# Two placements in a planned kernel: broadcast loads tied to tiles of x, and the sums of squares of the convolution at a lower rank

## The chip, the cores and the metric

One NeuronCore of a Trainium2 chip runs the whole program. Five engines have queues of their own and run them in order: TensorE (PE, with its weight loads PEld), VectorE (DVE), ScalarE (ACT), GpSimd (POOL) and SyncE (SP). SP mostly issues DMAs; POOL and ACT issue some as well. The metric is the device time of one execution in microseconds (us). The kernel before has a median of 1287.59 us over three runs.

## The reference, cut to what matters

One decoder layer on 1024 tokens of width 1024 in float32: a token mixer (sparse attention with 8 heads beside a short convolution) and a squared-ReLU MLP.

```python
h = rms_norm(x, g_mix_norm)
z = h @ w_in
q, kc, vc, ks_, vs_, kw_, vw_, gl, hc, cg, bg = split(z)
q = rms_norm(q, g_q)
k_cmp = rms_norm(compress(kc, pe_cmp[0], w_cmp1[0], b_cmp1[0], w_cmp2[0], b_cmp2[0]), g_k[0])
v_cmp = compress(vc, pe_cmp[1], w_cmp1[1], b_cmp1[1], w_cmp2[1], b_cmp2[1])
k_slc, k_win = rms_norm(ks_, g_k[1]), rms_norm(kw_, g_k[2])
attn_out = nsa_attention(q, k_cmp, v_cmp, k_slc, vs_, k_win, vw_, sigmoid(gl))
conv_out = bg * causal_conv3(cg * hc, conv_w)
mixed = concat(rms_norm(attn_out, g_out[:512]), rms_norm(conv_out, g_out[512:]))
x = x + mixed @ w_o
h = rms_norm(x, g_ffn_norm)
x = x + square(relu(h @ w_up)) @ w_down
```

Three things matter below. The vectors `g_q`, `g_k`, `b_cmp1` and `b_cmp2` are needed on every partition, since tokens lie on partitions where they are applied. `rms_norm(conv_out)` needs, for each token, the sum of the squares of its 512 convolution channels; its reciprocal root can be applied after the product with `w_o`. And nothing of the attention needs the convolution.

## The kernel before

**A plan ahead of the program.** The kernel doesn't issue instructions as its code runs. Each call such as `nc.tensor.matmul(...)` makes a node in a list (`Plan.op`), with the nodes that it must follow (those that wrote or read the same parts of the same tiles), an estimated cost, and a running number `n.k`. Allocating a tile and opening or closing a pool are nodes too, without an engine. `Plan.schedule` then runs a simulation of the five engines over the list: a node is ready when all that it follows has ended, and an engine that comes free takes its ready node of the highest priority. The priority is the longest path of estimated costs behind the node, less 0.03 for each place in the list, plus `plan.plus` as it stood when the node was made. `Plan.issue` emits the instructions in the order that comes out. So the plan fixes the order in each engine's queue. The waits on the chip are made from the tiles that instructions really share: an edge that exists only in the list moves an instruction in its queue, and nothing on the chip waits for it.

Tiles with the same tag share a ring of buffers. When the last node on a tile has ended in the simulation, its buffer goes into a heap, ordered by that time, and the next tile of the ring takes the first. All emitted instructions carry line 267 in the profile, the line where `Plan.op` calls the engine, so the profile is read by the names of tiles.

**The start.** `x` is loaded in eight tiles `xts` of 128 tokens (512 KB each, on SP), among the first pieces of `w_in` (also 512 KB). `norm_in` squares and sums a tile on ACT, takes the reciprocal root on DVE and POOL (`rs_t`, `ri`), scales the tile on DVE, and PE transposes it into `hTh` and `hTl`, a high and a low part for products of nearly float32 accuracy (`mm3`: three matmuls for one). POOL issues four loads that spread a vector over all partitions: `gq_bc` and `gk_bc` are written at the head of the code (lines 625 and 626), `b1_bc` and `b2_bc` after the keys' projection (lines 700 and 701). `gk_bc` is read when the first keys are normed (`kn`), `gq_bc` when queries are, `b1_bc` and `b2_bc` in the compression. In the profile `b1_bc` and `b2_bc` share the name `b_bc`; the one of 64 KB is `b2_bc`, the one of 256 KB `b1_bc`.

**The convolution and what follows.** Channels lie on partitions. For each of four blocks of 128 channels, three products `zc` run over two halves of 512 tokens; the result `cv` goes into `MCh`/`MCl`, and its square is added into `sqs[0]` or `sqs[1]`, one for each half. For the last block squares and additions run on DVE. Then eight matmuls with a vector of ones sum the squares over partitions, one for each 128 tokens (`ssc`, four from each `sqs`; the profile names this buffer `s__2825` and counts two instructions for each, 16 in all). `rsqrt` makes `rconv` of it on DVE (`rs_t`) and POOL.

Behind that stand the products `wc` of the convolution's part with `w_o`: 16 sums of 12 matmuls each, two for each block of 128 tokens, in the order of `ORDER` (blocks 3, 2, 1, 0 from the first half first). They rotate over three PSUM banks (tags `ot`, `ot`, `ms`). DVE multiplies each by its column of `rconv` and adds it to a tile of x (the group `y<-wc,rconv,y`), which frees the bank. Between them `k_transposes` turns the keys (`tp<-ident,kn`, four transposes a tile, three banks `pt`), and ACT and DVE split them into `KH` and `KL`. `queries` loads q again (`qx`) and turns it. `b2z.close()` gives the memory of `sqs` back, and a tile of x takes it later.

Of the kernel before, what the change touches and what calls it, by code (L numbers as in the profile page):

```python
# [16 lines left out]
DRAM = bass.MemoryType.DRAM  # L17

P = 128
# [131 lines left out]
class Plan:  # L151
# [27 lines left out]
    def pool(self, **kw):  # L179
        outer = self  # L180

        class Pool:
            def __enter__(self):
                self.bases, self.real, self.bufs = [], None, kw.get("bufs", 1)
                self.dram = kw.get("space") == DRAM
                self.psum = kw.get("space") == PSUM
                self.node = outer.pool_node(self.enter)
                return self

            def enter(self):  # L190
                self.real_pool = outer.tc.tile_pool(**kw)
                self.real = self.real_pool.__enter__()

            def __exit__(self, *a):
                if outer.done:
                    self.real_pool.__exit__(None, None, None)
                else:
                    n = outer.pool_node(lambda: self.real_pool.__exit__(None, None, None))
                    for b in self.bases:
                        n.preds.update(x.k for x in b.nodes + [b.node])  # L200
                    self.bases = None

            def tile(self, shape, dtype, name, tag=None, bufs=None):
                k = dict(name=name)
                if tag is not None:
                    k["tag"] = tag
                if bufs is not None:
                    k["bufs"] = bufs
                b = Base(self, shape, dtype, k)
                ring = outer.rings.setdefault((id(self), tag or name), [bufs or self.bufs])  # L210
                b.ring, b.node = ring, outer.node(None, [self.node])
                b.node.base = b
                if len(ring) > 1:
                    b.node.preds.add(ring[-1].node.k)
                ring.append(b)
                outer.bases.append(b)
                self.bases.append(b)

                def make():
                    b.tile = self.real.tile(shape, dtype, **k)  # L220
                b.node.do.append(make)
                return View(b, b.shadow, ())
        return Pool()

    done = False
# [8 lines left out]
    def op(self, name, engine, method, a, kw):  # L234
        views = [("" if i else "out", v) for i, v in enumerate(a)] + list(kw.items())
        views = [(k, v) for k, v in views if isinstance(v, View)]
        preds, raw, touched = set(), set(), []
        for k, v in views:
            w = k in ("out", "accum_out")
            r0, r1, m = v.region()  # L240
            touched.append((v.base, w, r0, r1, m))
            assert v.base.pool.bases is not None, v.base.kw
            preds.add(v.base.node.k)
            for n, ow, o0, o1, om in v.base.seen:
                if (w or ow) and r0 < o1 and o0 < r1 and m & om:
                    preds.add(n.k)
                    if ow:
                        raw.add(n.k)
        out = views[0][1] if views else None
        if name == "PE":  # L250
            preds.update([n.k for n in out.base.nodes if n.engine == "PE"][-1:])
        last = self.last_pe if name == "PE" else None
        if (last is not None and last.out is out.base and len(last.do) < self.GROUP and method == "matmul" and
                all(p <= last.k for p in preds)):
            node = last
            preds.discard(node.k)
        else:
            node = self.node(name)
            node.out = out.base if out is not None else None
        node.preds |= preds  # L260
        node.raw |= raw
        if name == "PE":
            self.last_pe = node

        def real(x):
            return x.real() if isinstance(x, View) else x
        node.do.append(lambda: getattr(engine, method)(*[real(x) for x in a], **{k: real(x) for k, x in kw.items()}))  # L267
        for b, w, r0, r1, m in touched:
            if b not in node.bases:
                b.nodes.append(node)  # L270
                node.bases.append(b)
            if w:
                b.seen = [s for s in b.seen if not (r0 <= s[2] and s[3] <= r1 and s[4] & ~m == 0)]
            b.seen.append((node, w, r0, r1, m))
        busy, late, size = self.cost(name, method, a, kw, views)
        node.plus = self.plus
        node.late = node.busy + late
        node.busy += busy
        node.port = self.port
        node.bytes += size  # L280
        node.names = method + " " + " ".join(v.base.kw["name"] for _, v in views)
        return node

    last_pe = None
    plus = 0.0
    GROUP = 1

    def cost(self, name, method, a, kw, views):
# [47 lines left out]
    def schedule(self, weight=lambda n: -.03 * n.k, rings=True):  # L336
        nodes = self.nodes
        slots, held, left_of = {}, {}, {}
        for b in self.bases:
            slots[id(b.ring)] = [(0.0, i, {}) for i in range(b.ring[0])]  # L340
            held[id(b.ring)] = []
            left_of[b] = [len(b.nodes), 0.0, {}]
            b.last = {x[0].k for x in b.seen if not x[1]} or {x[0].k for x in b.seen}
        for n in nodes:
            n.succ, n.left, n.ready = [], len(n.preds), 0.0
        for n in nodes:
            for p in n.preds:
                nodes[p].succ.append(n)
# [32 lines left out]
        def settle(n, t):  # L381
            for s in n.succ:
                s.left -= 1
                s.ready = max(s.ready, t + (.05 if s.engine and n.engine and s.engine != n.engine else 0.0))
                if not s.left:
                    stack.append(s)

        while True:
            while stack:
                n = stack.pop()  # L390
                if n.engine is None:
                    if n.base is not None:
                        ring = id(n.base.ring)
                        if not slots[ring]:
                            held[ring].append(n)
                            continue
                        t, _, n.users = heapq.heappop(slots[ring])
                        n.ready = max(n.ready, t)
                    order.append(n)
                    settle(n, n.ready)  # L400
                else:
                    heapq.heappush(wait[n.engine], (n.ready, n.k))
            best = None
            for e in names:
                if ready[e]:
                    t = free[e]
# [50 lines left out]
            for b in n.bases:  # L457
                rest = left_of[b]
                rest[0] -= 1
                rest[1] = max(rest[1], done)  # L460
                if n.k in b.last:
                    rest[2][n.line] = n
                if not rest[0]:
                    heapq.heappush(slots[id(b.ring)], (rest[1], 9 + b.node.k, rest[2]))
                    stack.extend(held[id(b.ring)])
                    held[id(b.ring)] = []
            for s in n.succ:
                s.left -= 1
                own = s.engine == e and not n.bytes and (e == "PE" or n.k not in s.raw)
                s.ready = max(s.ready, free[e] if own else done + .05 * (s.engine is not None))  # L470
                if not s.left:
                    stack.append(s)
        return end, order
# [14 lines left out]
def trunk_layer(ctx, tc, x, g_mix_norm, w_in, g_q, g_k, pe_cmp, w_cmp1, b_cmp1, w_cmp2, b_cmp2,  # L488
# [123 lines left out]
    with ExitStack() as a:  # L612
# [9 lines left out]
        nc.sync.dma_start(rows[24:36], conv_w.rearrange("j (k p) -> (j k) p", p=P))  # L622
        nc.sync.dma_start(rows[36:68], pe_cmp.rearrange("k (q two) d -> (k q) (two d)", two=2))
        plan.plus = 0.0
        nc.gpsimd.dma_start(gq_bc, g_q.partition_broadcast(P))
        nc.gpsimd.dma_start(gk_bc, g_k.partition_broadcast(P))
        tp = psB.tile([P, 512], F32, name="tp", tag="tr", bufs=3)
        nc.tensor.transpose(tp[:, :68], rows, ident[:68, :68])
        nc.vector.tensor_copy(cols, tp[:, :68])
# [17 lines left out]
        norm_in(0)  # L647
        kv_pieces = w_chunk(C_KV, 512)
        for tb in range(2, NT):
            nc.sync.dma_start(xts[tb], x2d[tb * P:(tb + 1) * P])  # L650
        for tb in range(1, NT):
            norm_in(tb)

# [14 lines left out]
    with ExitStack() as b1:  # L668
# [28 lines left out]
        cp = pool(cs, "cp", side="right")  # L697
        b1_bc = cp.tile([P, 2, 256], F32, name="b1_bc")
        b2_bc = tlp.tile([P, 2, HD], F32, name="b2_bc")
        nc.gpsimd.dma_start(b1_bc, b_cmp1.partition_broadcast(P))  # L700
        nc.gpsimd.dma_start(b2_bc, b_cmp2.partition_broadcast(P))

        def compress_steps():
            for kv in range(2):
# [120 lines left out]
    with ExitStack() as b2:  # L825
# [175 lines left out]
            return Qs  # L1001

        ssc = psS.tile([P, 512], F32, name="s_")[:, :NT]
        for tb in range(NT):
            nc.tensor.matmul(ssc[:, tb:tb + 1], sqs[tb // 4][:, (tb % 4) * P:(tb % 4 + 1) * P], ones,
                             start=True, stop=True)
        rsqrt(rconv, ssc, NT, 1.0 / CW)
        b2z.close()
        pts = [pool(kp_stack, "pt0")]
# [495 lines left out]
```

## Time and profile before

| | us |
|---|---|
| runs | 1282.5, 1287.59, 1288.23 |
| the profiled execution | 1286.31 |
| its span, first to last instruction | 1284.2 |
| PE busy in it | 1241.2 |
| DVE, ACT, POOL busy | 898.5, 691.3, 681.3 |

The profile is of one execution. A group shows busy time, the mean of one instruction and the idle time ahead of it with what ended that (the releaser). The chain of waits is the way back from the last instruction, at each step to what released it. A view by stretches shows for each the busy time of each engine, the granted PE clock (1.00 is full), the share of the 16 DMA engines in use and the GB/s they moved. In a row of the timeline stand start, length, engine, operation, output and inputs, the count of merged instructions, and the idle time before with its releaser in brackets. Matmuls overlap, so the length of one, 0.39 us at 512 columns, is longer than the distance from one start to the next.

### The profile page before, as it was taken

What the parts mean: (1) busy time and instruction counts of PE and PEld (TensorE: products, weight loads), DVE (VectorE), ACT (ScalarE), POOL (GpSimd) and SP (SyncE); (2) the same over time, 40 slices, a digit from 0 to 9 for tenths busy, and PEclk for the clock granted to TensorE, in tenths of its full rate; (3) what the DMA queues carried; (4) which work ended last, traced back from release to release, by engine and by line L of the source; (5) the groups of instructions that cost most, each with busy time, mean ns of one, the idle gap of its engine ahead of it and who ended that gap; (6) DMA issues with size and microseconds to landing.
All of it is one profiled execution on the core that took longest, in us unless ns stands there. A gap on an engine that the chain in (4) does not pass through costs nothing.

```text
span 1284.2 us, 18498 instructions
## 1 busy us (share of the span) xinstructions
PE 1241.2 (97%) x6170; PEld 1026.9 (80%) x6170; DVE 898.5 (70%) x1805; ACT 691.3 (54%) x1514; POOL 681.3 (53%) x599
## 2 busy tenths in 40 slices
PE   6999999999989999999999999999999999999998
PEld 5898888877768878888778878888877787888886
DVE  5367884433598788988885656656657998887875
ACT  6345552111499888887966554554434444444440
POOL 2255512120133332221586777777787989878861
PEclk9999999998999999999999999999999999999999
DMA  6243341212220010000415344355339654444413
GB/s 217 83 119 131 124 123 50 73 35 82 99 83 34 34 34 34 26 18 1 132 35 195 124 163 136 135 172 163 132 134 381 201 186 158 161 134 129 152 47 131
DMA packets 91574, 147.66 MB, mean 115 GB/s; under 512 B 10900, under 2 KB 45800, under 8 KB 91480
## 3 DMA queue, kind: packets, MB, share of 16 engines
q1 hardware_dynamic: 88408, 138.70, 32.6%
q10 hardware_dynamic: 2304, 5.24, 1.1%
q0 software_dynamic: 768, 2.56, 0.7%
q8 instruction: 48, 0.79, 0.3%
q14 instruction: 46, 0.38, 0.1%
HBM read 102.43 MB, written 44.04 MB: 114 GB/s over the span
## 4 chain that ended last, share of the span: by engine, by line
PE 84%; DVE 5%; ACT 5%; DMA 4%; issue 2%; POOL 0%; SPq 0%; DVEq 0%; ACTq 0%; POOLq 0%
PE X L267 24%; PE Z L267 15%; PE zc L267 10%; PE zp L267 8%; PE tp L267 6%; PE ot L267 4%; PE wc L267 3%; PE wa L267 3%; PE W L267 3%; DMA wu<-in_w_up_dram 1%; PE ops L267 1%; DVE y L267 1%; PE hp L267 1%; ACT pt L267 1%; ACT wu L267 1%
## 5 line engine op out<-in xcount | busy, mean ns | idle before, releaser
L267 PE MATMUL X<-we,uu 128*128 128x512 f32 x768 | 193.2, 393 | 5.7 <-ACT uu L267 4.0
L267 PEld LDWEIGHTS X<-we,uu 128*128 128x128 f32 x768 | 144.5, 189 | 39.3 <-ACT uu L267 8.1
L267 PE MATMUL Z<-we,uu 128*128 128x512 f32 x576 | 147.4, 391 | 0.6 <-DVE y L267 0.6
L267 ACT ACTIVATE uu<-ur 128x512 fp32r<-128x512 f32 x112 | 69.1, 631 | 123.3 <-PE X L267 62.2
L267 PEld LDWEIGHTS Z<-we,uu 128*128 128x128 f32 x576 | 107.2, 188 | 25.9 <-DVE y L267 2.4
L267 PE MATMUL tp<-ident,pt 128*128 128x128 f32 x528 | 100.8, 273 | 2.2 <-ACT pt L267 1.3
L267 POOL TENSOR_TENSOR d<-d 128x512 f32<-128x512 f32 x64 | 96.3, 1525 | 12.5 <-DVE d L267 11.3
L267 DVE TENSOR_TENSOR pl<-tp,ph 128x512 fp32r<-128x512 f32 (+1 forms) x148 | 95.2, 655 | 7.7 <-ACT ph L267 7.3
L267 ACT ACTIVATE pt<-pt,nm 128x640 f32<-128x640 f32 (+7 forms) x128 | 93.9, 736 | 9.7 <-DVE nm L267 9.3
L267 ACT ACTIVATE ph<-tp 128x512 fp32r<-128x512 f32 (+1 forms) x148 | 82.8, 575 | 19.6 <-PE tp L267 13.9
L267 DVE TENSOR_TENSOR y<-X,y 128x512 f32<-128x512 f32 x128 | 79.6, 680 | 15.9 <-PE X L267 15.3
L267 ACT ACTIVATE w_hi<-w_raw,cols 128x128 fp32r<-128x128 f32 (+3 forms) x128 | 54.0, 490 | 66.1 <-PE zc L267 48.9
L267 POOL TENSOR_TENSOR uu<-ur,uu 128x512 fp32r<-128x512 f32 x56 | 78.3, 1403 | 15.2 <-DVE y L267 10.7
L267 DVE TENSOR_TENSOR we<-s,we 128x512 fp32r<-128x512 f32 x42 | 39.3, 935 | 59.0 <-ACT we L267 27.5
L267 DVE TENSOR_TENSOR uu<-ur,uu 128x512 fp32r<-128x512 f32 x56 | 66.2, 1187 | 20.1 <-ACT uu L267 19.1
L267 PEld LDWEIGHTS tp<-ident,pt 128*128 128x128 f32 x528 | 67.9, 140 | 13.9 <-ACT pt L267 2.7
L267 DVE SCALAR_TENSOR_TENSOR w_lo<-w_raw,cols,w_hi 128x128 fp32r<-128x128 f32 (+3 forms) x128 | 61.6, 525 | 23.6 <-ACT w_hi L267 23.4
L267 DVE TENSOR_TENSOR y<-Z,y 128x512 f32<-128x512 f32 x96 | 61.3, 683 | 23.7 <-PE Z L267 23.7
L267 ACT ACTIVATE wu<-wu,cols 128x256 f32<-128x256 f32 x128 | 55.5, 504 | 23.2 <-DMA wu<-in_w_up_dram 21.7
L267 POOL TENSOR_TENSOR osb<-osb,ot_s 128x256 f32<-128x256 f32 x64 | 49.3, 770 | 34.9 <-DVE ot_s L267 29.9
L267 ACT ACTIVATE we<-wu 128x512 fp32r<-128x512 f32 x57 | 35.7, 632 | 58.6 <-PE X L267 45.8
L267 DVE SCALAR_TENSOR_TENSOR d<-d 128x512 f32<-128x512 f32 x48 | 64.9, 1353 | 0.9
(1261 smaller groups left out, 3592.5 us busy)
## 6 DMA issues: line engine op xcount, KB each, us to landing
u_d<-d SPq DMA_DIRECT2D x112, 256.0 KB, 4.1
ur<-u_d SPq DMA_DIRECT2D x112, 256.0 KB, 2.7
wu<-in_w_up_dram SPq DMA_DIRECT2D x16, 1024.0 KB, 5.5
wd<-in_w_down_dram SPq DMA_DIRECT2D x16, 1024.0 KB, 5.6
w_raw<-in_w_in_dram SPq DMA_DIRECT2D x20, 512.0 KB, 3.8
xt<-in_x_dram SPq DMA_DIRECT2D x10, 512.0 KB, 8.8
w_raw<-in_w_cmp_dram SPq DMA_DIRECT2D x8, 512.0 KB, 4.0
q_d<-qn SPq DMA_DIRECT2D x8, 512.0 KB, 2.9
```

The source lines that it names most:

```text
L267: node.do.append(lambda: getattr(engine, method)(*[real(x) for x in a], **{k: real(x) for k, x in kw.items()}))
```

## The change

Four edits. `plan.follow` is new: nodes in it are added to the predecessors of each node made while it is set. The loads of `gq_bc` and `gk_bc` move in the code to behind the load of x tile 5 (the sixth) and follow it; `b1_bc` and `b2_bc` follow the last load of x, tile 7. The eight matmuls of `ssc` get `plan.plus = -10`. In the simulation the heap of free buffers breaks ties by the last node on a buffer instead of by the tile's place, each node records what made it ready last (`cause`), the constant .05 gets the name `LINK`, and a term that was always zero leaves `settle`.

```diff
-                self.dram = kw.get("space") == DRAM
+                self.name, self.dram = kw["name"], kw.get("space") == DRAM
...
+        node.preds.update(p.k for p in self.follow)
...
+    follow = ()
+    LINK = .05
...
-            slots[id(b.ring)] = [(0.0, i, {}) for i in range(b.ring[0])]
+            slots[id(b.ring)] = [(0.0, -1, i, {}) for i in range(b.ring[0])]
...
-                s.ready = max(s.ready, t + (.05 if s.engine and n.engine and s.engine != n.engine else 0.0))
+                if t > s.ready:
+                    s.ready, s.cause = t, n.cause
...
-                    heapq.heappush(slots[id(b.ring)], (rest[1], 9 + b.node.k, rest[2]))
+                    heapq.heappush(slots[id(b.ring)], (rest[1], n.k, b.node.k, rest[2]))
...
-                s.ready = max(s.ready, free[e] if own else done + .05 * (s.engine is not None))
+                t = free[e] if own else done + self.LINK * (s.engine is not None)
+                if t > s.ready:
+                    s.ready, s.cause = t, n.k
...
-        nc.gpsimd.dma_start(gq_bc, g_q.partition_broadcast(P))
-        nc.gpsimd.dma_start(gk_bc, g_k.partition_broadcast(P))
...
-            nc.sync.dma_start(xts[tb], x2d[tb * P:(tb + 1) * P])
+            last = nc.sync.dma_start(xts[tb], x2d[tb * P:(tb + 1) * P])
+            if tb == 5:
+                plan.follow = (last,)
+                nc.gpsimd.dma_start(gq_bc, g_q.partition_broadcast(P))
+                nc.gpsimd.dma_start(gk_bc, g_k.partition_broadcast(P))
+                plan.follow = ()
...
+        plan.follow = (last,)
         nc.gpsimd.dma_start(b1_bc, b_cmp1.partition_broadcast(P))
         nc.gpsimd.dma_start(b2_bc, b_cmp2.partition_broadcast(P))
+        plan.follow = ()
...
+        plan.plus = -10.0
         for tb in range(NT):
             nc.tensor.matmul(ssc[:, tb:tb + 1], sqs[tb // 4][:, (tb % 4) * P:(tb % 4 + 1) * P], ones,
                              start=True, stop=True)
+        plan.plus = 0.0
```

More of the change, by code (lines that the diff above doesn't have):

```diff
@@ L344, in schedule @@
         for n in nodes:
-            n.succ, n.left, n.ready = [], len(n.preds), 0.0
+            n.succ, n.left, n.ready, n.cause = [], len(n.preds), 0.0, None
         for n in nodes:
@@ L396, in schedule @@
                             continue
-                        t, _, n.users = heapq.heappop(slots[ring])
-                        n.ready = max(n.ready, t)
+                        t, last, _, n.users = heapq.heappop(slots[ring])
+                        if t > n.ready:
+                            n.ready, n.cause = t, last
                     order.append(n)
```

## The prediction

> **What bounds the kernel now.** I read the head of the page first, then busy time by stretches, then each place where TensorE (PE) idles.
>
> ```profile
> span 1284.2 us, 18498 instructions
> PE 1241.2 (97%) x6170; PEld 1026.9 (80%) x6170; DVE 898.5 (70%) x1805; ACT 691.3 (54%) x1514; POOL 681.3 (53%) x599
> PEclk9999999998999999999999999999999999999999
> ...
> PE 84%; DVE 5%; ACT 5%; DMA 4%; issue 2%; POOL 0%; SPq 0%; DVEq 0%; ACTq 0%; POOLq 0%
> ```
>
> PE is busy 97% of the span and carries 84% of the chain that ended last. Its idle time is 1284.2 - 1241.2 = 43 us; an edit that only moves work can win no more, unless matmuls themselves run quicker. One clock digit of 40 is an 8, so such a place exists. By stretches (PE's busy time is the second number; behind POOL stands the granted clock):
>
> ```profile
> 0.00:14.00 14.00, 2.39 (x10) 1.83 (x11) 2.25 (x10) 5.44 (x10) 4.19 (x20) 1.00 0.79 239
> ...
> 14.00:60.00 46.00, 46.00 (x218) 38.27 (x219) 28.22 (x59) 25.91 (x53) 10.05 (x17) 1.00 0.38 125
> 60.00:283.00 223.00, 221.38 (x1119) 188.74 (x1118) 132.39 (x339) 87.36 (x221) 76.23 (x76) 1.00 0.31 93
> 283.00:345.00 62.00, 59.51 (x287) 48.69 (x286) 27.74 (x64) 14.37 (x36) 10.67 (x16) 0.94 0.24 81
> 345.00:760.00 415.00, 399.95 (x2316) 332.74 (x2315) 330.10 (x885) 324.22 (x785) 180.81 (x194) 1.00 0.20 68
> ```
>
> PE idles 11.6 us before 14, not at all up to 60, 1.6 up to 283, 2.5 up to 345 and 15 in the attention. The change acts in the first row and in the fourth. Between 14 and 345 PE hardly stops, so what it gains at either place is still there at 345.
>
> **Part 1: three loads leave the start.** The prices first:
>
> ```profile
> 1.31 0.70 POOL L267 DMA_DIRECT2D gk_bc<-in_g_k_dram  x1 [0.36 <-issue]
> 2.54 0.58 POOL L267 DMA_DIRECT2D gq_bc<-in_g_q_dram  x1
> 3.22 0.54 POOL L267 DMA_DIRECT2D b_bc<-in_b_cmp_dram  x1
> 21.38 0.55 POOL L267 TENSOR_TENSOR ri<-rs_t,mhalf 128x1 f32<-128x1 f32 x1 [3.32 <-DVE rs_t L267]
> 38.75 0.61 DVE L267 SCALAR_TENSOR_TENSOR kn<-z,kri,gk_bc 128x128 f32<-128x128 f32 x2 [0.83 <-POOL kri L267]
> ...
> 3.03 7.99 DMA xt<-in_x_dram
> ...
> DMA to landing us min/median/max: 3.7/8.8/10.9
> ...
> q0 software_dynamic: 112, 0.20, 21.7%
> ...
> 4.00:5.00 1.00, 0.00 (x0) 0.00 (x0) 0.00 (x0) 0.52 (x1) 0.10 (x1) 1.00 0.67 77
> 11.00:12.00 1.00, 0.00 (x0) 0.00 (x0) 0.00 (x0) 0.89 (x1) 0.00 (x0) 1.00 1.01 406
> 24.00:26.00 2.00, 2.00 (x15) 1.70 (x14) 1.65 (x5) 2.00 (x4) 0.69 (x2) 1.00 0.00 0
> ```
>
> The chain runs through the second tile of x: issued at 3.03, it lands 7.99 us later, and ACT, DVE, POOL and PE wait for it. While it is under way the DMA engines are 0.67 full but move 77 GB/s; at 11 us they are full and move 406. In those first 12 us the queue of the POOL loads (the q0 row is of that stretch: packets, MB, share) held 21.7% of 16 engines with 0.20 MB: 12 x 0.217 = 2.6 us of all of them. Best case: the second tile takes the 3.7 us of the quickest, which wins 7.99 - 3.7 = 4.3 us. Worst case: nothing is won, since tiles of x take 8.8 us at the median, and two POOL issues stand just ahead of a norm's reciprocal and hold it 0.70 + 0.58 = 1.3 us. I take **2.6 us won**, the engine time itself, the row nearest to the thing priced. The third tile and the weights come over the same engines and move along.
>
> Where the loads go: the edges to tiles of x exist in the list alone; on the chip the loads merely stand later in POOL's queue. They were ready from the start; made to follow the sixth tile, gk_bc and gq_bc should fall near the reciprocal at 21.38, before which POOL idles 3.32 us, more than the 1.3 of issue. b2_bc and b1_bc follow the eighth tile; b1_bc stands behind the last norm already. Behind them in POOL's queue wait only the reciprocals of the remaining tiles, and for those DVE and then PE. The transfers then share with the last tiles and weights, but the queues are empty at 24 to 26, so 2.6 us more fit. gk_bc is first read at 38.75. Without that cover the 1.3 us come back on the norms.
>
> **Part 2: the sums of squares rank last.** The eight matmuls of ssc (s__2825 here) in two groups:
>
> ```profile
> 283.15 0.95 PE L267 MATMUL s__2825<-ones,sqs 128*128 128x1 f32 x8
> 286.81 0.39 PE L267 MATMUL wc<-w_hi,MCh 128*128 128x512 f32 x1
> 288.94 0.69 DVE L267 TENSOR_TENSOR sqs<-sqs,cv 128x512 f32<-128x512 f32 x1
> 289.69 1.86 PE L267 MATMUL s__2825<-ones,sqs 128*128 128x1 f32 x8 [2.50 <-DVE sqs L267]
> 291.58 0.17 DVE L267 TENSOR_SCALAR rs_t<-s__2825 128x8 f32<-128x8 f32 x1 [1.95 <-PE s__2825 L267]
> 291.84 1.65 POOL L267 TENSOR_TENSOR rconv<-rs_t,mhalf 128x8 f32<-128x8 f32 x1 [1.73 <-DVE rs_t L267]
> 294.88 0.68 DVE L267 TENSOR_TENSOR KL<-tp,KH 64x512 fp32r<-64x512 f32 x1 [3.12 <-ACT KH L267]
> 296.82 1.41 DVE L267 SCALAR_TENSOR_TENSOR y<-wc,rconv,y 128x512 f32<-128x512 f32 x2 [1.26 <-PE wc L267]
> ...
> 289.00:290.00 1.00, 0.31 (x2) 0.31 (x2) 0.63 (x1) 0.00 (x0) 1.00 (x2) 0.86 0.00 0
> 290.00:291.00 1.00, 1.00 (x7) 1.00 (x6) 0.00 (x0) 0.00 (x0) 0.11 (x1) 0.50 0.00 0
> ...
> 296.00:297.00 1.00, 1.00 (x5) 0.72 (x5) 0.18 (x1) 0.00 (x0) 0.00 (x0) 0.72 0.00 0
> ...
> 28.17 3.66 PE zp L267 x16
> 31.83 0.87 PE tp L267 x8
> ```
>
> The second group stands in PE's queue ahead of wc matmuls and transposes and holds PE 2.50 us until the squares are summed. Then PE runs at half clock from 289.86 to 296.7: lost are 0.14 + 6 x 0.50 + 0.28 = 3.4 us. The stop costs 2.5 + 3.4 = 5.9 us.
>
> Ten us less priority puts these matmuls behind all that the two open wc sums and the first transposes hold: a sum's 12 matmuls are a path of 2.7 us, and rs_t with rconv makes the path of ssc only 1.8 longer than a sum's last matmul. So from 283.15 PE runs 24 wc matmuls (3.66 / 16 = 0.229 each, 5.5 us), ten transposes (0.87 / 8 each, 1.1) and the first group (0.95): it is at the second group at 290.7, after the squares' end at 289.63. No wait is left there. What is late next: the fourth tile of transposes needs a bank that KL frees (0.68, behind the squares on DVE, so 290.3, against 289.7 on PE), 0.6 us; and rconv, at best 0.17 + 1.65 behind sums that end near 293, lets the first product (1.41 for two) free a bank at 295.8, with the 0.26 between rs_t and rconv. PE has by then done the third sum's rest and six transposes (1.8 + 0.7, to 295.5); the stop is 0.3, with the other gaps between engines 0.5. That is 1.1 of new stops: **5.9 - 1.1 = 4.8 us won**. Bounds: 5.9, and nothing, if the stop of 2.5 with its half clock returns at rconv. One SP entry, a tile of x into the squares' memory, waits for ssc and gets some 1.5 us later.
>
> The Trainium skill, "TensorE: Matmul & The Clock Gate", Part 1, says that about 3.4 us of idleness halves the clock and 3.4 us of sustained work restores it. Here 2.50 us of idleness did, with the thin matmuls around it, and half clock lasted 6.9 us. By the rule alone a stop this short would cost its 2.5 us only, and the sum would be 7.4 - 3.4 = 4.0; the trace of before decides for before, and what is left of the question is rival F.
>
> The new tie-break of free buffers, the recorded causes and LINK (.05 as before) issue nothing. Two places in the count of nodes shift priorities by 0.06, too little but for ties; what a reordered rest may do is left to the rivals.
>
> **Sum.** 2.6 + 4.8 = 7.4 us. The profiled execution took 1286.31 (its span and 2.1 around it), so it becomes 1278.9; it lies 1.28 under the median 1287.59, so the median becomes **1280.2**.
>
> **The rivals.**
>
> ```profile
> PE X L267 <- ACT uu L267: 4.0, 2, 2.7
> PE ops L267 <- ACT oTs L267: 2.6, 6, 0.8
> PE Z L267 <- ACT d L267: 2.3, 4, 1.4
> PE tpq L267 <- DMA qx<-q_d: 1.8, 2, 1.3
> ...
> qx<-q_d SPq DMA_DIRECT2D x16, 256.0 KB, 2.6
> ```
>
> (B) The stop comes back at rconv: the sums go behind the third wc sum too, all banks stand full, PE waits 0.17 + 1.65 and a product, about 2.5 us, and the clock halves again. For it: nothing else ranks near them. Against it: at equal order the third sum's path is the shorter. Part 1 alone is left: 1287.59 - 2.6 = 1285.0, no change.
>
> (C) Slower: the list behind ssc is made anew, and in SP's queue the loads of q (16, 2.6 us each) slip behind loads that wait for memory freed later. Place: the head of each of the eight query blocks, where PE waits for q now twice, 1.8 us in all. Price: a stop that halves the clock, 5.9 us. Two of them, 11.8 - 7.4, are still under the bound; from the third on it is slower: 17.7 - 7.4 = +10.3, 1297.9. Against it: 2.6 us is short beside a block's 415 / 8 = 52.
>
> (D) Part 1 wins nothing: the loads lay beside waits that last anyway, tiles of x taking 8.8 us without them too, or they fall in POOL's queue so that they still meet the first tiles, the list's edge not being one of the chip. 1287.59 - 4.8 = 1282.8. The Trainium skill, "DMA: Bandwidth & Descriptors", Rules for kernel authors, speaks for this one: issue a load early and wait for it late. The trace has both loads waited for by nobody, as that rule wants, beside a tile that was late.
>
> (E) Faster still: the new order also loses half of the three first waits above, (4.0 + 2.6 + 2.3) / 2 = 4.4: 1275.8. Nothing in the change aims there.
>
> (F) The clock halves even without the long stop, since in both groups PE does thin matmuls for 0.95 and 1.86 us beside short stops. 3.4 us come back: 1283.6, no change. Against it: after the first group, at 283.96, no half clock is to be seen.
>
> **Numbers.** Forecast 0.45, B 0.10, C 0.22, D 0.07, E 0.12, F 0.04. The forecast's own range is 1276 to 1284: both best bounds (4.3 + 5.9 = 10.2) give 1277.4, and a little below that for the spread of runs; half of the 7.4 lost gives 1283.9. No change means within 0.5%, which is about what a measurement of this kernel can tell: 1281.15 to 1294.0. Faster: two thirds of the forecast (0.30), E, and 0.03 of D: 0.45. Slower: C, 0.22. No change: the rest, 0.33. The range takes in B, D, E, F and one or two of C's stops: 1274 to 1293.
>
> **What would show it.** Right: the second tile of x lands near 8.4 instead of 11.02; no PE wait for sqs; granted clock 1.00 from 283 to 300; 36 wc matmuls and the thin ones done by 296. Wrong: POOL's loads ahead of 12 us; a PE stop of 2 us or more before a wc matmul, with a clock of 0.50 behind it; PE idle after 345 over 20 us.

## The result, and the profile after

The changed kernel took 1280.62 us (median of seven runs, 1279.77 to 1283.21); the kernel before took 1288.23 (seven runs, 1282.5 to 1290.22) beside it. The ratio of the two series is 0.9951, with a 95% interval of 0.9931 to 0.997: 0.5% faster, or 6.3 us of 1288.23 (3.9 to 8.9). The two medians alone differ by 7.6 us. The forecast was 1280.2. The profiled execution took 1283.21, the slowest of the seven; its span is 1281.1, 3.1 less than before.

The head of its page, its first lines and the chain by engine:

```profile
span 1281.1 us, 18498 instructions
PE 1241.3 (97%) x6170; PEld 1028.4 (80%) x6170; DVE 896.0 (70%) x1805; ACT 691.0 (54%) x1514; POOL 680.0 (53%) x599
PEclk9999999999999999999999999999999999999999
PE 83%; DVE 5%; DMA 4%; ACT 4%; issue 2%; POOL 1%; DVEq 0%; ACTq 0%; SPq 0%; POOLq 0%
```

PE is busy as long as before (1241.2), so the 3.1 us less of span are 3.1 us less of idle time: 1281.1 - 1241.3 = 39.8 instead of 43.0. The same stretches as before (columns: stretch, length, busy time and instructions of PE, PEld, DVE, ACT, POOL, granted clock, DMA share, GB/s):

```profile
0.00:14.00 14.00, 5.21 (x20) 4.11 (x21) 5.50 (x15) 8.11 (x14) 2.96 (x18) 1.00 0.80 280
14.00:60.00 46.00, 46.00 (x225) 38.41 (x224) 25.26 (x55) 23.60 (x51) 11.30 (x19) 1.00 0.39 123
60.00:283.00 223.00, 220.76 (x1110) 188.22 (x1110) 132.77 (x341) 87.66 (x223) 76.92 (x79) 0.99 0.31 91
283.00:345.00 62.00, 59.16 (x294) 49.07 (x293) 28.48 (x71) 16.81 (x40) 10.62 (x16) 0.96 0.31 97
345.00:760.00 415.00, 403.22 (x2324) 336.13 (x2324) 331.40 (x878) 324.79 (x786) 182.82 (x193) 1.00 0.21 70
```

At the start PE works 5.21 us instead of 2.39. But the third row has a clock of 0.99 where it had 1.00, and the fourth only 0.96 where it had 0.94: half clock has gone from one place in part and come to another. The start in the timeline of the changed kernel, with the same matmul of the kernel before in the fence behind it:

```profile
5.00 0.47 SPq L268 DMA_DIRECT2D xt<-in_x_dram  x1
7.25 1.06 ACT L268 ACTIVATE junk<-xt 128x1024 bf16<-128x1024 f32 x1 [1.51 <-DMA xt<-in_x_dram]
12.09 0.80 PE L268 MATMUL zp<-w_hi,hTh 128*128 128x512 f32 x1 [0.91 <-ACT w_hi L268]
14.50 0.55 POOL L268 TENSOR_TENSOR ri<-rs_t,mhalf 128x1 f32<-128x1 f32 x1 [3.74 <-DVE rs_t L268]
15.04 0.71 POOL L268 DMA_DIRECT2D gk_bc<-in_g_k_dram  x1
15.75 0.55 POOL L268 DMA_DIRECT2D gq_bc<-in_g_q_dram  x1
18.82 0.56 POOL L268 TENSOR_TENSOR ri<-rs_t,mhalf 128x1 f32<-128x1 f32 x1 [2.51 <-DVE rs_t L268]
19.34 0.94 POOL L268 DMA_DIRECT2D b_bc<-in_b_cmp_dram  x1
```

```profile
15.54 0.78 PE L267 MATMUL zp<-w_hi,hTh 128*128 128x512 f32 x1
```

The second tile of x is read at 7.25 instead of about 11, and the first projection matmul starts 15.54 - 12.09 = 3.45 us earlier. The three loads that stood at the start are now issued at 15.04 to 19.34, behind reciprocals, and POOL is idle again before the next one (2.51): nobody waits behind them. The place of the sums, again in the timeline:

```profile
287.65 0.69 DVE L268 TENSOR_TENSOR sqs<-sqs,cv 128x512 f32<-128x512 f32 x1
288.26 0.67 DVE L268 TENSOR_TENSOR KL<-tp,KH 64x512 fp32r<-64x512 f32 x1
288.99 0.55 PE L268 MATMUL tp<-ident,kn 128*128 128x128 f32 x3 [0.68 <-DVE KL L268]
289.37 0.95 PE L268 MATMUL s__2825<-ones,sqs 128*128 128x1 f32 x8
290.19 0.49 PE L268 MATMUL wc<-w_hi,MCh 128*128 128x512 f32 x1
290.51 0.28 PE L268 MATMUL s__2825<-ones,sqs 128*128 128x1 f32 x2
```

No wait for `sqs` is left. PE stops 0.68 us, for KL, does the first group of four sums (eight instructions) in one piece and the second one sum (two instructions) at a time, between matmuls of the third wc sum. The clock in four-microsecond windows of the same execution, and among them the first full microsecond at half clock:

```profile
76.00:80.00 4.00, 4.00 (x23) 3.99 (x22) 2.61 (x8) 3.06 (x11) 2.35 (x4) 0.61 0.05 12
292.00:293.00 1.00, 1.00 (x6) 0.82 (x5) 0.17 (x1) 0.00 (x0) 0.46 (x1) 0.50 0.39 156
292.00:296.00 4.00, 4.00 (x17) 3.31 (x16) 1.81 (x4) 1.69 (x3) 1.65 (x1) 0.59 0.68 187
344.00:348.00 4.00, 4.00 (x21) 3.58 (x20) 3.12 (x11) 3.53 (x9) 0.00 (x0) 0.69 0.60 177
```

Three places ran at half clock for a while. 4 x (1 - 0.61) = 1.6 us are lost near 76, about 1.6 again at 292 (before it was 3.4), and 1.2 in the last window, whose half clock begins already at 343.1, ahead of the window; over its whole length each place lost 1.7. The first stands behind a stop of 1.9 us, in the list of waits:

```profile
PE tp L268 <- DMA ch<-kv_d: 1.9, 1, 1.9
```

**Where the gain went, step by step.** The first projection starts 3.45 us earlier. The squares end 288.94 - 287.65 = 1.29 earlier: the half clock near 76 and a stop for `ch` that is longer by 0.3 (1.9 instead of 1.6) took most of the difference. The last wc matmul, in the timelines of before and after:

```profile
343.13 0.40 PE L267 MATMUL wc<-w_hi,MCl 128*128 128x512 f32 x1
```

```profile
338.08 0.40 PE L268 MATMUL wc<-w_hi,MCl 128*128 128x512 f32 x1
1273.80 1.07 PE L268 MATMUL Z<-we,uu 128*128 128x512 f32 x4
```

It comes 5.05 earlier, so the second part won 5.05 - 1.29 = 3.8 here. The last matmul ends at 1274.87 instead of 1279.17, 4.3 earlier, and the span is shorter by 3.1: what stands behind the last matmul, the last stores, takes 6.2 us instead of 5.0.

### The profile page after: what moved, and what is told of

Read it like the earlier page. It is cut to its first block, busy times and chain, and to the rows that moved or that the text cites. A ratio compares the mean times of both kernels' runs of the same rounds, so it can differ in the third digit from the quotient of the medians.

```text
span 1281.1 us, 18498 instructions
## 1 busy us (share of the span) xinstructions
PE 1241.3 (97%) x6170; PEld 1028.4 (80%) x6170; DVE 896.0 (70%) x1805; ACT 691.0 (54%) x1514; POOL 680.0 (53%) x599
## 4 chain that ended last, share of the span: by engine, by line
PE 83%; DVE 5%; DMA 4%; ACT 4%; issue 2%; POOL 1%; DVEq 0%; ACTq 0%; SPq 0%; POOLq 0%
PE X L268 23%; PE Z L268 15%; PE zc L268 10%; PE zp L268 8%; PE tp L268 6%; PE ot L268 5%; PE wa L268 3%; PE wc L268 3%; PE W L268 3%; DMA wu<-in_w_up_dram 2%; PE ops L268 1%; DVE y L268 1%; PE hp L268 1%; ACT wu L268 1%; DVE we L268 1%
## 5 line engine op out<-in xcount | busy, mean ns | idle before, releaser
L268 PE MATMUL zc<-hTl,w_hi 128*128 128x512 f32 x192 | 65.3, 389 | 0.0
```

## The experiments

All ratios are to the kernel before, run on the same chip in the same series; medians in us. Where no other base is named, a diff is against the changed kernel.

**One part at a time.** First the loads alone:

```diff
-        plan.plus = -10.0
+        plan.plus = 0.0
         for tb in range(NT):
             nc.tensor.matmul(ssc[:, tb:tb + 1], ...
```

> The changed kernel with the sums of squares at their old rank, so only the loads move. Theory (two parts that add up): the second tile of x lands near 7.2 us and the first zp matmul starts near 12.1 us, as in the changed kernel; the stop of 2.5 us at the sums of squares and some 6 us of half clock behind it are there as before; the time is 2.5 to 3.5 us under the kernel before, ratio 0.997 to 0.998. Rival (the start is given back further on): the first zp matmul starts early, but the end of the convolution products is within 1 us of before, ratio 0.9995 or more.

Measured: 1285.27 beside 1288.59, ratio 0.9974 (0.996 to 0.9988). Its timeline:

```profile
8.03 1.06 ACT L268 ACTIVATE junk<-xt 128x1024 bf16<-128x1024 f32 x1 [2.46 <-DMA xt<-in_x_dram]
11.66 0.79 PE L268 MATMUL zp<-w_hi,hTh 128*128 128x512 f32 x1
```

The start is like that of the changed kernel, 3.9 us ahead of before, and in its list of waits the old one of 2.5 us for `sqs` is back. Then the rank alone, with the loads at their old places:

```diff
+        nc.gpsimd.dma_start(gq_bc, g_q.partition_broadcast(P))
+        nc.gpsimd.dma_start(gk_bc, g_k.partition_broadcast(P))
...
-            if tb == 5:
-                plan.follow = (last,)
...
-        plan.follow = (last,)
         nc.gpsimd.dma_start(b1_bc, b_cmp1.partition_broadcast(P))
```

> The changed kernel with the loads where they were, so only the sums of squares rank lower. Theory: the second tile of x lands near 11 us, PE doesn't wait for the squares, and the time is 3.5 to 5 us under the kernel before, ratio 0.996 to 0.9975; at most a short half clock after the thin matmuls. Rival (the stop only moves to the reciprocal root): a PE wait of 2 us before a wc matmul near 296 and a ratio of 0.999 or more.

Measured: 1284.82, ratio 0.9967 (0.9952 to 0.9981). Its first zp matmul is at 15.45, as before, and no wait for `sqs` is left. So each part wins by itself, 0.26% (3.3 us, interval 1.5 to 5.2) and 0.33% (4.3, interval 2.4 to 6.2), and together they come to 0.9974 x 0.9967 = 0.9941, inside the interval of the changed kernel. As far as these intervals tell, neither hangs on the other.

**Is it the transfers, or the list?** Leaving the loads away from the start also gives 13 of PE's instructions there another place in the list. This kernel keeps all of the change and adds three loads of the same vectors at the start, which nobody reads:

```diff
+        plan.plus = 600.0
+        nc.gpsimd.dma_start(xp.tile([P, 3, HD], F32, name="idle_k", bufs=1), g_k.partition_broadcast(P))
+        nc.gpsimd.dma_start(xp.tile([P, HD], F32, name="idle_q", bufs=1), g_q.partition_broadcast(P))
+        nc.gpsimd.dma_start(xp.tile([P, 2, HD], F32, name="idle_b", bufs=1), b_cmp2.partition_broadcast(P))
+        plan.plus = 0.0
```

> The changed kernel with three loads more at the start, of the sizes of the three that left it, into tiles that nobody reads; the loads of the change stay late. Theory (the loads' company made the second tile late): it lands near 11 us again, the first zp matmul starts near 15.4 us, and the time is 2.5 to 3.5 us over the changed kernel, about 1283.5 to 1284. Rival (what helped was the order of POOL's own work, its constants and reciprocals): the tile lands near 7.2 us and the time stays at 1280.6.

Measured: 1286.07, ratio 0.9982 (0.9965 to 0.9999). In its timeline the start is that of before again, though nobody waits for the added loads:

```profile
11.88 1.06 ACT L268 ACTIVATE junk<-xt 128x1024 bf16<-128x1024 f32 x1 [6.22 <-DMA xt<-in_x_dram]
15.50 0.79 PE L268 MATMUL zp<-w_hi,hTh 128*128 128x512 f32 x1
```

PE, DVE and ACT go through the same list of tiles in the same order as in the changed kernel, so it isn't the list: the transfers, or their issue, held the second tile. The time is higher than the 1283.5 to 1284 expected, and its interval overlaps that of the rank alone (0.9952 to 0.9981), whose start it has.

**The changed kernel again,** unaltered, for the spread of its clock:

> The changed kernel once more, for a second trace. Theory (after a stop of about 2 us the clock halves or not as it falls): the places of half clock near 76, 293 and 343 us aren't all the same in this execution, and the time follows them at 1.5 to 2 us a place. Rival (the halving belongs to the program): the same three places.

Measured: 1282.31 in one run. Its windows:

```profile
76.00:80.00 4.00, 4.00 (x34) 3.95 (x33) 2.67 (x9) 3.38 (x11) 2.89 (x4) 1.00 0.29 67
288.00:292.00 4.00, 4.00 (x21) 3.54 (x20) 0.17 (x1) 0.00 (x0) 0.76 (x1) 0.66 0.56 137
292.00:296.00 4.00, 4.00 (x14) 3.13 (x13) 2.80 (x5) 1.68 (x3) 0.90 (x1) 0.50 0.69 212
344.00:348.00 4.00, 4.00 (x18) 3.51 (x17) 2.86 (x11) 3.58 (x11) 0.00 (x0) 0.59 0.52 160
```

The same program, in another execution, keeps full clock near 76, although its stop for `ch` there is longer, as its list of waits has it,

```profile
PE tp L268 <- DMA ch<-kv_d: 2.3, 1, 2.3
```

and loses 4 x (0.34 + 0.50) = 3.4 us at the sums, as much as the kernel before. Where the clock halves is thus not settled by the length of a stop alone; the last section comes back to this.

**Again, timed in five rounds:**

> The changed kernel, timed beside the next three. Theory: the two parts alone gave ratios of 0.9974 and 0.9967, and they add up, 0.994 (1281). Rival (they share a gain): not under 0.996.

Measured: 1279.51 beside 1287.39, ratio 0.9933 (0.9907 to 0.9958). The half clock at 292 is there as in the first profile (0.60 in the window from 292 to 296), and so is the one near 76.

**Are the thin matmuls to blame?** The sums are written 64 columns wide instead of one, against a vector of ones read 64 times; the reciprocal root takes the first column:

```diff
-        ssc = psS.tile([P, 512], F32, name="s_")[:, :NT]
+        ssc = psS.tile([P, 512], F32, name="s_").rearrange("p (t c) -> p t c", t=NT)
...
-            nc.tensor.matmul(ssc[:, tb:tb + 1], sqs[tb // 4][:, (tb % 4) * P:(tb % 4 + 1) * P], ones,
+            nc.tensor.matmul(ssc[:, tb], sqs[tb // 4][:, (tb % 4) * P:(tb % 4 + 1) * P], ones.to_broadcast([P, 64]),
...
-        rsqrt(rconv, ssc, NT, 1.0 / CW)
+        rsqrt(rconv, ssc[:, :, 0], NT, 1.0 / CW)
```

> The changed kernel with each sum of squares over 64 equal columns of ones instead of one (the same sums, 64 times; one is read). Theory (the thin matmuls count as near idleness, and with the stop of 0.7 us they let the clock fall): no half clock near 293, and a time 0 to 1.7 us under the changed kernel. Rival (the stop alone, or chance): half clock near 293 in the trace, and the same time. If the wide sums cost more than thin ones, PE's spacing of them over 0.12 us shows it.

Measured: 1278.51, ratio 0.9931 (0.9906 to 0.9955), not told apart from the unaltered kernel in the same series (0.9933). Its profile has no half clock from 283 to 300, but neither has that of the three idle loads, with thin sums. One profile each decides nothing where executions differ as the last two did: inconclusive. A group of four wide sums takes 1.00 us where the thin one takes 0.95, so the width costs next to nothing either way.

**Later still.** The rank goes from -10 to -30:

```diff
-        plan.plus = -10.0
+        plan.plus = -30.0
```

> The changed kernel with the rank lowered by 30 instead of 10: the sums stand behind the third wc sum and all transposes of keys but four. Theory: PE now has nothing left while the reciprocal root is made, a stop of 2 to 3 us before a wc matmul or a transpose, often with half clock behind it; the time is 2 to 6 us over the changed kernel. Rival (a lower rank can only help, since PE has transposes and queries to do): no such stop, and the time of the changed kernel.

Measured: 1282.9, ratio 0.9961 (0.9946 to 0.9976), 0.28% above the changed kernel of the same series, though the two intervals overlap. The stop comes, but at the first scores of the attention (timeline, then a window):

```profile
297.44 0.63 PE L268 MATMUL s__2826<-KH,Qg 128*128 128x320 f32 x1 [0.69 <-ACT Qg L268]
299.37 0.63 PE L268 MATMUL s__2826<-KL,Qz 128*128 128x320 f32 x1 [1.09 <-POOL Qz L268]
...
298.00:300.00 2.00, 0.91 (x4) 0.63 (x3) 1.21 (x2) 0.00 (x0) 1.31 (x2) 0.50 1.02 412
```

PE has run out of wc sums whose banks can be freed and starts on scores whose inputs are not there: 0.69 + 1.09 us of stops, and half clock from 297 to 304. So -30 is too late a rank by what the trace shows, and -10 is short of that.

**What is it about three loads?** Five kernels add idle loads at the start of the changed one, in the way of the three above. One alone, `g_k`, 96 KB, issued at 1.28:

> The changed kernel with one load more at the start, 96 KB of the 192 that left it. Theory (the time on the DMA engines counts, half of it): the second tile of x lands near 9.3 us, the first zp matmul starts near 13.5 us, and the time is some 1.5 us over the changed kernel. Rival (any one POOL load is enough, by its own delay): near 11 us, 15.4 us and 3 us.

Measured: 1280.72, ratio 0.9936 (0.9914 to 0.9959). The second tile is read at 8.27 and zp starts at 11.87. In the three profiles of the changed kernel these are 7.25, 8.34 and 8.24, and 12.09, 11.96 and 11.83. So there is no delay, and neither of the two outcomes expected. One of 32 KB (`g_q`), at the same moment:

> The changed kernel with one idle load of g_q at the start: 32 KB in rows of 256 B. Theory A (short rows are slow: the 96 KB load took 4.1% of 16 engines in 12 us, the two short ones together 16%): the second tile of x lands 1 to 2 us later than the 7.2 to 8.2 of the changed kernel, near 9.5. Theory B (it is the loads that come second and third in POOL's queue, beside the second tile): it is the first now, so no delay. Time: under 1.5 us over the changed kernel in either case.

Measured: 1280.94, ratio 0.9937 (0.9916 to 0.9958); the second tile at 8.00. One of 64 KB (`b_cmp2`):

> The changed kernel with one idle load of b_cmp2 at the start: 64 KB in rows of 512 B. Theory A (short rows): the second tile of x near 9.5 us. Theory B (place in the queue): no delay. If e9 delays and this doesn't, or the other way round, it is the one load and not its kind.

Measured: 1281.99, ratio 0.9939 (0.9915 to 0.9963); the second tile at 7.93. None of the three vectors is harmful by itself, whatever its rows. Three loads of `g_k`, the first at 1.28, all issued by 3.07:

> The changed kernel with three idle loads of g_k at the start: 288 KB in rows of 768 B, half as much again as the 192 KB that left. Theory A (short rows): 3 x 4.1% of 12 us is 1.5 us of the engines, the second tile of x lands before 9.5 us and the time is within 1.5 us of the changed kernel. Theory B (second and third in the queue): the tile lands near 11 to 12 us as in the run with three idle loads, and the time is 3 us over. The bytes alone would say the same as B.

Measured: 1286.12, ratio 0.9973 (0.9955 to 0.999); the second tile at 11.07, zp at 15.84, the delay of before. It is left to tell the number of loads from their moment. The last kernel has one load of `g_k`, issued later, behind a memset on POOL (of memory that is overwritten; on PE the 13 places at the start stand as in the kernel before):

```diff
+        plan.plus = 600.0
+        nc.gpsimd.memset(us[1][:, 2:1026], 0.0)
+        plan.plus = -55.0
+        nc.gpsimd.dma_start(xp.tile([P, 3, HD], F32, name="idle_k", bufs=1), g_k.partition_broadcast(P))
+        plan.plus = 0.0
```

> The changed kernel with one idle load of g_k, 96 KB, that POOL issues at about 2.5 us instead of 1.3, behind a memset of 1024 columns that is added ahead of it (into memory that is written again later). Theory (the moment counts: what POOL issues near 2 to 3 us shares the engines with the second tile of x, which is issued at 3.0): the second tile lands at 9.5 us or later and the time is 1 to 3 us over the changed kernel. Rival (the number counts: one POOL load is harmless at any moment, and only a row of them is slow): the tile lands near 8 us, as with the one early load.

Measured: 1282.15, ratio 0.9947 (0.993 to 0.9965). The timeline of the early load, with the row of the POOL queue in the first 12 us (packets, MB, share of 16 engines) and that of the load (size, us to landing):

```profile
1.28 0.70 POOL L268 DMA_DIRECT2D idle_k<-in_g_k_dram  x1 [0.82 <-POOLq L1508]
8.27 1.06 ACT L268 ACTIVATE junk<-xt 128x1024 bf16<-128x1024 f32 x1 [2.61 <-DMA xt<-in_x_dram]
...
q0 software_dynamic: 48, 0.10, 4.1%
idle_k<-in_g_k_dram POOLq DMA_DIRECT2D x1, 96.0 KB, 3.8
```

The same rows of the late one:

```profile
2.42 0.72 POOL L268 DMA_DIRECT2D idle_k<-in_g_k_dram  x1
10.02 1.06 ACT L268 ACTIVATE junk<-xt 128x1024 bf16<-128x1024 f32 x1 [4.50 <-DMA xt<-in_x_dram]
...
q0 software_dynamic: 48, 0.10, 12.5%
idle_k<-in_g_k_dram POOLq DMA_DIRECT2D x1, 96.0 KB, 6.3
```

The same 48 packets hold the engines three times as long when they are issued 1.14 us later, land in 6.3 us instead of 3.8, and the second tile, whose load SP issues at 3.02 in both, is read 1.75 us later. By the times alone the late load is not told apart from the early ones (0.9947 beside 0.9936 to 0.9939). The early load lands at 1.28 + 3.8 = 5.1, so it too is under way together with the second tile for some 2 us. What differs is when its packets are on the engines: all 48 from 3.6 to 4.7 us in the early run, but 45 of the 48 from 4.7 to 8.4 in the late one. A reading that fits all these starts is that a load of POOL costs by the packets that it still has on the engines behind some 4.7 us; until then the first tile, which ACT reads at 4.4 to 4.6, is still landing. One late load does some half of what three do, so the number may count beside the moment; and why the packets are then so slow, no run shows.

## Why the prediction was right, step by step

**Part 1, 2.6 us for three loads gone from the start.** Right in the place and the direction: the second tile is read at 7.25 to 8.34 in the three profiles of the changed kernel (8.4 forecast), the first two loads stand behind 12 us in the gap ahead of the reciprocal at 18.82, which was the one at 21.38, as forecast, and nothing behind them waits. Loads alone won 3.3 us by the times, with an interval that holds 2.6; the trace has 3.45 at the first zp matmul. A little small, then, and still under the best bound of 4.3. What failed is the reason given for the size, the time that the loads held the engines. One load at 1.28 held 12 x 0.041 = 0.5 us and cost nothing; the same load at 2.42 held 12 x 0.125 = 1.5 and delayed the tile 1.75. The engine time is itself an outcome of the collision, so that 2.6 came near the measured gain is partly luck. Rival D, that the start wins nothing, fell with the loads alone and with the three idle ones. The Trainium skill, "DMA: Bandwidth & Descriptors", Rules for kernel authors, which stood behind D, says to issue early and wait late, so that the fixed setup cost overlaps. These runs agree with it for the single load at 1.28, which cost nothing. The rule does not price what a load costs its neighbours: three loads that nobody waited for took back some 0.35% (0.9973 beside 0.9937 and 0.9939 of the single ones).

**Part 2, 4.8 us for the sums.** The steps came as told: no wait for `sqs`; the wc matmuls, the transposes and the first group ahead; the second group among the third sum's matmuls; a new stop for KL of 0.68 (0.6 forecast). The stop of 0.5 put at rconv did not come. By the stops and half clock of the two profiles, 2.50 + 3.4 before stands against 0.68 + 1.7 after: 3.5, and 3.8 by the ledger, where 4.8 was forecast. The term that was mis-sized is the half clock, taken as gone for good: 1.7 of its 3.4 came back in this execution and in the timed repeat, and all 3.4 in the single run between them. Ten profiles of these runs have the thin sums at rank -10. At the sums five of them lost nothing, four 1.7 us and one 3.4, 1.0 on average; the two profiles with the old rank lost 3.4 each. With 1.0 in the place of nothing, and 0.68 of new stops, the part comes to 5.9 - 0.68 - 1.0 = 4.2. By the times the rank alone won 4.3, with an interval that holds all these figures. So rival F, given 0.04, came true, in part or whole, in half of these profiles, and the mark "clock 1.00 from 283 to 300" failed in the profiled one. The prediction also misread where the half clock of before lies (289.73 to 296.56, not 289.86 to 296.7); the loss of 3.4 is right.

**The sum.** 7.4 was forecast, 6.3 and 8.6 (1287.39 x 0.0067) were measured in two series. That the median fell 0.4 us from the forecast is closer than either can tell, and luck in part: the parts alone won 3.3 and 4.3 where 2.6 and 4.8 were forecast, and the two misses nearly cancel.

**The other rivals.** B, the stop that comes back, needs the sums at a later rank; at -30 it came, at the scores and not at rconv, for about 3.6 us (0.28% of 1287) and not the 4.8 forecast. C and E wanted a reordered rest of the list. By the names of tiles in the two traces, only 117 of 6170 instructions on PE and 2 of 371 DMAs on SP stand at another place, at the start and around the sums; the loads of q didn't move. The tie-break, the recorded causes and LINK have no run of their own. The loads alone, run with them, move just 13 of PE's places, all at the start, and the rank alone, also with them, the other 104. One mark was badly set: "PE idle after 345 over 20 us" holds for the kernel before already (by stretches, 939.00 - 911.95 = 27.1 from 345 to 1284; after it is 936.00 - 910.20 = 25.8 to 1281).

## What to carry to other kernels

A load that nobody waits for is not free: look at which transfer on the chain is issued in the same microsecond, and move the one with slack by a few instructions of its queue; price it by the moment of its neighbour, not by its bytes. Work that is short but waits for a late input belongs behind what is ready, but only so far that its own successors don't run dry. And where half clock adds to a stop, count the stop as the sure gain and the clock as one that comes back in a share of the executions.

## What the runs showed of the hardware

A program of this kind has half clock at different places in different executions. In the changed kernel's three profiles the stop near 76 halved the clock behind 1.9 and 2.1 us and not behind 2.3, and the sums lost 1.7, 3.4 and 1.7 us. Losses come in two sizes everywhere: behind the first 20 us, every stretch of half clock that lies wholly inside one of the 14 spans is 3.41 or 6.83 us long and so loses 1.7 or 3.4. Within one execution all of them begin a whole number of steps of 3.413 us apart. In the first profile they begin at 76.85, 291.89, 343.09 and 960.90 us, which is 63, 78 and 259 steps behind the first; in the next execution of the same program the steps lie elsewhere (289.27, 343.89, 961.70). The Trainium skill, "TensorE: Matmul & The Clock Gate", Part 1, describes a free-running window of 3413 ns that doesn't start with the kernel; the traces agree with it. The records of the clock begin only at 15.4 us in the first profile and at 20.1 in that of before, and ahead of that the views print 1.00. Yet matmuls of zp start 0.43 us apart there and 0.23 behind it, so PE begins at half clock too, and the 1.00 of the first rows is not to be trusted.

These windows explain why the shorter stop counted and the longer one didn't. Two windows in a row near 76, in the first profile and then in the next execution (columns as before):

```profile
73.44:76.85 3.41, 1.49 (x14) 1.46 (x13) 0.76 (x2) 0.20 (x1) 0.00 (x0) 1.00 0.18 24
76.85:80.26 3.41, 3.41 (x17) 3.40 (x16) 2.11 (x8) 3.12 (x11) 2.61 (x4) 0.50 0.13 29
```

```profile
70.82:74.23 3.41, 1.80 (x14) 1.57 (x13) 0.00 (x0) 0.00 (x0) 0.00 (x0) 1.00 0.91 148
74.23:77.65 3.42, 2.78 (x23) 2.81 (x24) 1.58 (x3) 1.54 (x6) 0.54 (x1) 1.00 0.02 5
```

The stop of 1.9 us fell into one window and left PE busy for 1.49 / 3.41 = 0.44 of it; half clock followed. The stop of 2.3 us was cut in two by a window's edge, 1.80 / 3.41 = 0.53 was left, and none followed. Cut into such windows from 20 us on, the 14 traces have 25 at full clock and without thin sums in which PE was busy for 0.44 or less, and half clock followed all of them. It followed two of the five from 0.45 to 0.46 and none above, but for windows that hold thin sums. There, in the ten profiles at rank -10, PE was busy for 0.79 to 0.92 of the window in which the stop for KL ends; half clock followed the five that held 12 to 16 of the 16 thin instructions, and not the five that held 3 to 10. So at the sums the place of a window's edge decided between executions with the same stop, and the thin instructions seem to count for little in it. That last step is read off ten profiles; no experiment here shows it. The wide sums don't settle it, since their 16 instructions fell into a window that holds nothing of the stop.

The Trainium skill, "TensorE: Matmul & The Clock Gate", Part 1, also says that a whole window of idleness halves the clock. That does not fit: half clock followed windows in which PE was busy for 0.08 to 0.46, the one above with a stop of 1.9 us among them, and at the sums windows with a stop of 0.7 or less.

The other surprise is the early load: 96 KB spread over the partitions cost nothing at 1.28 us and 1.75 us of a neighbour's arrival at 2.42.
